# Moving the output blocks of two column tiles forward among the matmuls of a fused matmul and batch norm

## The chip, the cores and the metric

One core of a Trainium2 chip. The metric is the device time of one execution in microseconds (us); medians of several executions are quoted. Engines: PE is TensorE (matmuls and matmul transposes), DVE is VectorE, ACT is ScalarE, POOL is GpSimd, SP is SyncE, which issues the stores.

## The reference

```python
# x: 16 x 512 x 1024, weight: 1024 x 768, all float32
y = np.matmul(x, weight)                       # 8192 rows, 768 columns
mean = np.mean(y, axis=(0, 1), keepdims=True)  # per column, over all rows
var = np.var(y, axis=(0, 1), keepdims=True)
y_norm = (y - mean) / np.sqrt(var + eps)
return gamma * y_norm + beta
```

A column can be written only when all its 8192 rows are known. The kernel therefore works by column tiles of 128 (nt 0 to 5): a tile is multiplied, its statistics are closed, and it goes out while the next tiles are multiplied.

## The kernel before: the parts concerned

Rows come in 16 chunks of 512 (C = 16). The first phase loads x and computes nt 0 to 2 for all rows and nt 3 to 5 for the first five chunks (EARLY). After that nothing is loaded; nt 3, 4 and 5 are multiplied one after the other for the other eleven chunks. A result of nt 3 to 5 lies transposed (columns on the partitions), so it has to be normalised, turned back by PE, copied out of PSUM and stored. A block is two chunks: 1024 rows of one column tile, 512 KB.

```python
    def mm(nt, c, jws=range(JW), q0=0, q1=QPC):
        # [cut: bank]
        for jw in jws:
            for e in range(2):
                seq(nc.tensor.matmul(y_ps, w_sb[...], xT[c][...], ...))
                if turns:
                    turn_one()          # one waiting transpose after each matmul

    def finish(nt):
        seq(nc.vector.bn_aggr(mv[:, nt, :], stats[:, nt, :, :]))
        seq(nc.scalar.activation(std[:, one], mv[:, nt, 1:2], AF.Sqrt, bias=eps_sb, scale=1.0))
        # [cut: reciprocal, scale, shift]

    def out_copy(nts, m0, eng, late=False):
        while any(k == (nts, m0) for k, _, _ in turns):
            turn_one()                  # what is left of the block's 8 transposes, in a row
        # [cut: source; the target is a place in the ring, or an xT buffer when late]

    def outputs(nt, t0, step):
        for b in range(C // 2):
            tb = t0 + step * b
            for i in range(2):
                at(tb - 1.4 + 0.5 * i, norm, nt, 2 * b + i, "act" if tb < tr + 2.0 else "dve")
            at(tb, turn_y, (nt,), 2 * b * CH, 2 * RT)        # queue 8 transposes
            at(tb + 2.2, out_copy, (nt,), 2 * b * CH, "act")
            at(tb + 2.3, store, (nt,), 2 * b * CH, 2 * RT)

    for nt in range(GA, NT):            # GA = 3
        for c in range(EARLY, C):
            for jws in halves:
                unit(nt, c, MM_US / 2 + (0.12 if nt == GA else 0.17), jws)
        at(pe + 0.55, finish, nt)
        if nt == GA:
            outputs(nt, S + 40.0, 2.2)
        elif nt < NT - 1:
            outputs(nt, max(pe + 4.0, S + 55.0), 2.0)
        else:
            last_outputs(nt, pe + 3.0)
```

`at(t, ...)` gives a piece of work a planned time. All pieces are sorted by that time, and the sorted list is the order of instructions of each engine. The times are a plan only: on the chip an engine takes its instructions in that order, each as soon as what it waits for is there. `S` is the planned end of the first phase, `pe` the planned end of the tile's matmuls, `tr` the planned end of the row outputs of nt 0 to 2, which DVE and POOL normalise. The rule `tb < tr + 2.0` gives the earlier normalisations to ACT. The ring is one SBUF buffer for the data of most stores; a new piece waits until the store that used its place has landed.

## Time and profile before

| | before |
|---|---|
| median of the first runs | 223.6 us (223.54 to 223.75) |
| last matmul starts | 198.6 us |
| last copy out of PSUM ends | 212.5 us |
| last store lands | 220.3 us |

PE is busy without a hole up to the last matmul; the end is a queue of stores. Most lines of the profile that show this stand in the prediction. One more of the page, from its list of DMA issues (count, size, median us from issue to landing), is that of the last tile's large stores:

```profile
out_dram<-o_sb SPq DMA_DIRECT2D x7, 512.0 KB, 5.9
```

A lone store of that size lands after 2.9 us; the other 3.0 us it stands behind two more stores of 1.5 us each.

### The profile page before, as it was taken

To read this page: it belongs to the slowest core of one execution; us is meant where nothing else is said; L and a number is where in the kernel's file an instruction comes from. 1 tells how busy PE (TensorE), PEld (TensorE's weight loads), DVE (VectorE), ACT (ScalarE), POOL (GpSimd) and SP (SyncE) were. 2 spreads that over 40 slices of the span, in tenths; PEclk is the share of its full clock that TensorE was granted. 3 is DMA by queue.
4 is the path that set the end of the run, shared out by engine and by line. 5 is a ranking of instruction groups with operands and counts; after the bars stand their busy time and mean duration, and the time that the engine had idled before them with its cause. 6 is when DMAs were issued, how large, how long until landed. Compare 5 with 4: busy or idle time off the path is not lost.

```text
span 221.4 us, 3354 instructions
## 1 busy us (share of the span) xinstructions
PE 201.3 (91%) x1166; PEld 104.0 (47%) x1166; DVE 150.9 (68%) x260; ACT 117.5 (53%) x207; POOL 122.5 (55%) x145
## 2 busy tenths in 40 slices
PE   7669999999999999999999999999999999996510
PEld 3344555444545456465465544454444555555300
DVE  3222878897778888888634389778977568558930
ACT  2001553533554556465466217878879976858500
POOL 8897595964678689655069005996999300003000
PEclk9979999999999999999999999999999999997965
DMA  5999999999999999990000002898899998978995
GB/s 60 176 197 175 196 196 196 197 197 196 194 190 196 197 195 196 196 182 4 0 0 4 0 0 104 320 337 312 310 340 341 330 272 254 302 228 260 346 347 164
DMA packets 70049, 43.74 MB, mean 198 GB/s; under 512 B 3984, under 2 KB 69520, under 8 KB 70032
## 3 DMA queue, kind: packets, MB, share of 16 engines
q0 software_dynamic: 34624, 18.36, 60.6%
q1 hardware_dynamic: 35408, 25.18, 35.2%
q8 instruction: 9, 0.15, 0.3%
q14 instruction: 8, 0.07, 0.1%
HBM read 36.71 MB, written 25.17 MB: 280 GB/s over the span
## 4 chain that ended last, share of the span: by engine, by line
PE 84%; DMA 4%; DVE 3%; ACT 2%; issue 1%; POOL 1%; DVEq 0%; ACTq 0%; POOLq 0%
PE y_ps L189 52%; PE y_ps L179 23%; PE o_ps L336 7%; DMA ring<-in_x_dram 4%; DVE o_sb L351 1%; ACT o_sb L349 1%; POOL ring L155 1%; DVE y_sb L320 1%; ACT y_sb L315 1%; PE a_ps L262 1%; PE tot_ps L225 1%; ACT ring L349 0%; DVE xT_sb L167 0%; DVE stats L295 0%; ACT y_sb L298 0%
## 5 line engine op out<-in xcount | busy, mean ns | idle before, releaser
L189 PE MATMUL y_ps<-xT_sb,w_sb 128*128 128x512 bf16 (+1 forms) x540 | 133.0, 386 | 3.8 <-DVE xT_sb L167 1.9
L189 PEld LDWEIGHTS <-w_sb 128*128 128x128 bf16 x540 | 52.0, 97 | 69.7 <-issue 5.8
L295 DVE BATCH_NORM_STATS2 stats<-y_ps 128x6 f32<-128x512 f32 x66 | 45.0, 689 | 32.0 <-PE y_ps L189 31.8
L298 ACT CAST y_sb<-y_ps 128x512 bf16<-128x512 f32 x66 | 38.7, 586 | 52.2 <-DVE stats L295 49.5
L155 POOL DMA_DIRECT2D ring<-in_x_dram x72 | 45.3, 635 | 14.1 <-DVE xT_sb L167 7.4
L179 PE MATMUL y_ps<-w_sb,xT_sb 128*128 128x384 bf16 x320 | 53.1, 326 | 0.0
L336 PE MATMUL o_ps<-ident,y_sb 128*128 128x128 bf16 x264 | 45.5, 227 | 4.9 <-DVE y_sb L320 2.6
L167 DVE STREAM_TRANSPOSE xT_sb<-ring 128x1024 f32<-128x1024 f32 (+1 forms) x34 | 39.3, 1167 | 12.1 <-DMA ring<-in_x_dram 12.1
L205 POOL TENSOR_TENSOR sum<-sum,sq_sb 128x384 f32<-128x384 f32 x32 | 32.1, 1003 | 22.5 <-ACT sq_sb L201 21.3
L276 POOL TENSOR_TENSOR ring<-ring,sum 128x768 f32<-128x768 f32 x20 | 36.1, 1843 | 15.2 <-DVE ring L270 14.9
L179 PEld LDWEIGHTS <-xT_sb 128*128 128x128 bf16 x320 | 31.3, 98 | 21.6
L349 ACT CAST ring<-o_ps 128x1024 f32<-128x1024 bf16 (+1 forms) x28 | 25.8, 925 | 12.6 <-ACT y_sb L298 5.9
L208 DVE TENSOR_TENSOR sum<-y_ps,sum 128x384 f32<-128x384 f32 x40 | 21.8, 546 | 13.7 <-ACT sq_sb L201 13.1
L336 PEld LDWEIGHTS <-y_sb 128*128 128x128 bf16 x264 | 22.9, 101 | 9.9 <-DVE y_sb L320 6.0
L201 ACT ACTIVATE sq_sb<-y_ps 128x384 f32<-128x384 f32 x40 | 19.5, 493 | 13.1 <-PE y_ps L179 10.7
L214 ACT CAST y_sb<-y_ps 128x384 bf16<-128x384 f32 x40 | 19.0, 476 | 6.4 <-DVE sum L208 6.2
L270 DVE TENSOR_TENSOR ring<-y_sb,a_ps 128x768 f32<-128x768 bf16 x20 | 18.7, 938 | 0.0
L320 POOL TENSOR_SCALAR y_sb<-y_sb,scale,shift 128x512 bf16<-128x512 bf16 x2 | 1.7, 846 | 28.0 <-DVE shift L309 28.0
L315 ACT ACTIVATE y_sb<-y_sb,shift,scale 128x512 bf16<-128x512 bf16 x21 | 16.3, 816 | 0.0
L320 DVE TENSOR_SCALAR y_sb<-y_sb,scale,shift 128x512 bf16<-128x512 bf16 x43 | 16.1, 424 | 0.0
L148 PE MATMUL idle_ps<-idle_sb 128*128 128x512 bf16 x26 | 7.1, 441 | 1.2 <-DVE idle_sb L99 1.2
L142 POOL DMA_DIRECT2D w_sb<-in_weight_dram x12 | 6.1, 513 | 0.5 <-issue 0.2
(47 smaller groups left out, 36.3 us busy)
## 6 DMA issues: line engine op xcount, KB each, us to landing
ring<-in_x_dram POOLq DMA_DIRECT2D x56, 256.0 KB, 8.7
out_dram<-ring SPq DMA_DIRECT2D x32, 384.0 KB, 3.3
out_dram<-ring SPq DMA_DIRECT2D x16, 512.0 KB, 3.0
out_dram<-o_sb SPq DMA_DIRECT2D x7, 512.0 KB, 5.9
ring<-in_x_dram POOLq DMA_DIRECT2D x16, 128.0 KB, 5.2
w_sb<-in_weight_dram POOLq DMA_DIRECT2D x8, 96.0 KB, 4.5
w_sb<-in_weight_dram POOLq DMA_DIRECT2D x4, 192.0 KB, 5.1
out_dram<-o_sb SPq DMA_DIRECT2D x2, 256.0 KB, 4.7
```

Source lines behind the costliest of these rows:

```text
L155: seq(nc.gpsimd.dma_start(x_bf[32 * i:32 * i + 32], src[:, :, KQ * i:KQ * (i + 1)]))
L167: seq(nc.vector.transpose(dst[:, half, :, jw0:jw1], src[:, :, jw0:jw1]))
L179: seq(nc.tensor.matmul(y_ps, xT[c][:, jw, s * P:(s + 1) * P, e], w_sb[:, jw, e, 0:NA], start=(jw == 0 and e == 0), stop=(jw == JW - 1 and ...
L189: seq(nc.tensor.matmul(y_ps, w_sb[:, jw, e, nt * P:(nt + 1) * P], xT[c][:, jw, q0 * QR:q1 * QR, e], start=(jw == 0 and e == 0 and q0 == 0) ...
L205: seq(eng.tensor_add(acc, acc, py.pop(("sq", c, s))))
L208: seq(nc.vector.tensor_add(sum1, py["row", c, s][:, 0:NA], sum1))
L276: seq(nc.gpsimd.tensor_add(o_sb, o_sb, sum1[:, None, :].to_broadcast([P, 2, NA])))
L295: seq(nc.vector.bn_stats(stats[:, nt, i, :], py[nt, c]))
L298: seq(nc.scalar.copy(y(nt, c), py.pop((nt, c))))
L320: seq((nc.vector if eng == "dve" else nc.gpsimd).tensor_scalar(y(nt, c), y(nt, c), scale[:, nt:nt + 1], shift[:, nt:nt + 1], op0=ALU.mult, ...
L336: seq(nc.tensor.transpose(dst, src, ident))
L349: seq(nc.scalar.copy(o_sb, src))
```

## The change

The outputs of nt 3 begin 4 us of plan earlier and at closer steps; those of nt 4 begin right after its statistics, 6.5 us of plan earlier, and thus overlap those of nt 3. The intent: more of the transposes and stores lie beside matmuls, and less is left for the end.

```diff
         if nt == GA:
-            outputs(nt, S + 40.0, 2.2)
+            outputs(nt, S + 36.0, 1.95)
         elif nt < NT - 1:
-            outputs(nt, max(pe + 4.0, S + 55.0), 2.0)
+            outputs(nt, pe + 3.6, 1.85)
```

## The prediction

> **What bounds the kernel now.** I read the page's busy line first, then a table of stretches, the waits, the chain of work that ended last, and last the timelines of ScalarE (ACT) and of the stores. Three stretches matter: 162 to 178 us, where the outputs of the fourth column tile (nt 3) begin; 178 to 199 us, up to the last matmul; and the end.
>
> ```profile
> PE 201.3 (91%) x1166; PEld 104.0 (47%) x1166; DVE 150.9 (68%) x260; ACT 117.5 (53%) x207; POOL 122.5 (55%) x145
> ...
> 162.00:170.00 8.00, 7.96 (x47) 3.71 (x46) 6.04 (x9) 6.86 (x12) 8.00 (x6) 1.00 0.97 358
> 170.00:178.00 8.00, 8.00 (x59) 4.32 (x58) 5.13 (x14) 7.91 (x13) 3.53 (x2) 1.00 1.00 345
> 178.00:199.00 21.00, 21.00 (x158) 11.51 (x156) 13.18 (x31) 14.59 (x20) 0.00 (x0) 1.00 0.86 259
> 199.00:205.00 6.00, 4.02 (x41) 3.14 (x38) 5.25 (x12) 4.64 (x8) 1.68 (x2) 0.74 0.89 266
> 205.00:222.00 17.00, 3.45 (x40) 2.26 (x40) 7.04 (x14) 2.99 (x3) 0.00 (x0) 0.70 0.91 274
> ```
>
> The columns of the stretches are length, then busy time of PE, PE weight loads, DVE, ACT and POOL, then granted clock, DMA share and GB/s. PE is busy without a hole to 199 us, so until there every matmul or transpose that is added moves the last matmul. ACT is full (7.91 of 8.00) from 170 to 178, and has room (14.59 of 21.00) after it. From 205 on no engine is full, but the DMA is: the chain of work and the stores show the end.
>
> ```profile
> PEld L336 <- ACT y_sb L315: 0.5, 2, 0.4
> ...
> 198.75 0.24 PE y_ps L189
> 199.02 0.70 DVE stats L295
> 199.72 0.31 DVE y_sb L320
> 200.03 0.51 DVE mv L302
> 200.56 0.30 ACT std L303
> 201.42 1.13 DVE y_sb L320 x2
> ...
> SPq L538 <- DMA out_dram<-o_sb: 4.2, 3, 1.5
> ...
> L354 SPq DMA_DIRECT2D out_dram<-o_sb x9: 522/1390/1719, 203.7 to 214.4; - x9
> ```
>
> The first line is what PE waits for ACT's normalisations today: 0.5 us. The next six are the last matmul, its statistics, one normalisation of nt 4 that stands between them and the aggregate, the standard deviation, and the first normalisation of the last tile (nt 5) at 201.42. The chain then goes through transposes and copies and ends with a copy at 212.5, nine microseconds before the end: the rest is stores. The nine stores of nt 5 are issued from 203.7 to 214.4, though the last copy was there at 212.5: an issue stretches to 1.4 us where 0.37 is usual. At the very end the stores land 1.5 us apart (4.2 us in 3 waits, longest 1.5). 512 KB (0.524 MB) in 1.5 us is 347 GB/s, the full rate of this window. Store by store, the last two of nt 4 (issued 202.27 and 203.19) land at 206.7 and 208.2, and those of nt 5 follow without a gap: 208.9, 209.7, 211.2, and so on every 1.5 us to 220.3. So the end is a DMA queue that begins with work of nt 4.
>
> ```profile
> 168.30 1.52 ACT L315 ACTIVATE y_sb<-y_sb,shift,scale 128x512 bf16<-128x512 bf16 x2
> 169.73 0.57 ACT L298 CAST y_sb<-y_ps 128x512 bf16<-128x512 f32 x1
> 170.19 1.53 ACT L315 ACTIVATE y_sb<-y_sb,shift,scale 128x512 bf16<-128x512 bf16 x2
> 171.62 0.57 ACT L298 CAST y_sb<-y_ps 128x512 bf16<-128x512 f32 x1
> 172.08 1.02 ACT L349 CAST ring<-o_ps 128x1024 f32<-128x1024 bf16 x1
> 172.99 1.53 ACT L315 ACTIVATE y_sb<-y_sb,shift,scale 128x512 bf16<-128x512 bf16 x2
> ```
>
> Read start to start, because instructions on ACT overlap at their ends: a normalisation (L315) holds ACT 0.715 us (1.43 for two), a copy out of a matmul bank (L298) 0.46, an output copy (L349) 0.91, and one of 768 columns 0.69.
>
> **What the Trainium skill says.** "TensorE: Matmul & The Clock Gate", Back-to-back issue gap, gives columns over 2.4 GHz plus 2.5 ns for a lone warm matmul, thus some 56 ns for 128 columns, and a slower 81 ns sustained with weight loads. In this trace a pair of a 512-column matmul and a transpose takes 0.281 us where the matmul alone takes 0.226: a transpose costs 0.055. Five transposes in a row between two matmuls take 0.50 less 0.226, also 0.055 each, so runs of them are no dearer here. "Advanced Engine Details and Errata", Sequencer Loop, has engine instructions pushed into a queue and waiting there for their semaphores; I read it as in order, and the trace agrees (at 164.33 a transpose that waits for ACT holds the matmul behind it, 0.43 us between starts). "DMA: Bandwidth & Descriptors", Anatomy of one DMA, gives a fixed cost of about 2.0 us plus bytes over 436 GB/s. The trace has 2.9 us for a lone store of 512 KB, 1.4 fixed and 1.5 for the bytes; I use the trace.
>
> **The change part by part.** No instruction's work is added or taken away; the order changes. I counted it in the built kernels.
>
> (a) Transposes of nt 4. Before, 17 of its 64 come after the last matmul, where they lie beside the statistics and cost nothing. After, all come before it, and the last 20 matmuls run bare. That is 17 x 0.055 = +0.94 us to the last matmul.
>
> (b) The normalisation of nt 4 between the last statistics and the aggregate is gone: -0.31.
>
> (c) ACT between 164 and 178 us. The rule that gives a normalisation to ACT depends on the planned time, so four more of nt 3's go to ACT (ten, not six); and up to nt 4's standard deviation two more output copies stand in its order. 4 x 0.715 + 2 x 0.91 = 4.7 us more work in a stretch where ACT has next to no room. I walked both orders side by side. ACT from 163.89, where the orders part, never idle: the normalisations of chunks 0 and 1 end at 166.1, chunk 2 at 167.3, chunk 3 at 168.7; then a bank copy and two output copies; chunk 4 at 171.5, chunk 6 at 174.3, chunk 8 at 177.1. PE: the first two blocks of transposes find their chunks ready. PE reaches the third block at 170.26 and waits for chunk 4 to 171.5: 1.25 us. Eight pairs later (2.25 us) it is at 173.8 and waits for chunk 6 to 174.35: 0.55. Then 176.6, and chunk 8: 0.55 again. Chunks 10 on are DVE's, ready in time. Sum about +2.35 us. As PE has no hole later, it isn't made good.
>
> (d) Buffers. The output ring is shared by all stores, so the order of its reuse changes. A store of row tiles is now behind the first store of nt 3 in SyncE's order, and lands some 2.5 us later; the last row normalisation on DVE waits for its place, I reckon from 170 to 174. DVE has idle time there, and the bank it should free isn't wanted for eight allocations. No cost.
>
> (e) The end. With nt 4's stores all landed, nt 5's find an empty queue. Relative to the statistics, the first copy may now start at once on ACT, which before was busy with two output copies of nt 4 till 203.16. In the old times the stores of nt 5 would be issued at 203.0, 203.65, 205.35, 206.0, 207.8, 208.15, 210.25, 210.6 and 212.6. Each lands 1.5 us (0.75 for the two small ones) after the later of the landing before it and its issue + 1.43. The third lands at 205.35 + 1.43 + 1.5 = 208.3, and six more at 1.5 us make 217.3, against 220.3: -3.0. The same rule gives the landings of before to 0.1 us.
>
> Sum: +0.94 - 0.31 + 2.35 - 3.0 = 0.0 us. The gain is real and is given back by PE.
>
> **The rivals.** First, ACT keeps up (the waits of (c) don't appear). For it: only some tenths of slack decide each wait, and the schedule was drawn up so that ACT's work should fit. Against it: 7.91 of 8.00 busy today. Then the sum is -2.4, 221.2 us. Second, the ACT queue is worse than I walked it: the output copies wait for ring places (the waits show ACT before L349 at a few tenths each), each wait delays the normalisations behind it, and PE pays one for one; 1.5 us more gives 225.1. Third, the DMA end is no better: an instruction fetch on one DMA engine at 202.9 lies in the old tail, where the store issued at 202.27 took 4.4 us to land and not 2.9. If it comes at the same place and holds nt 5's stores, 0.7 of the 3.0 is lost, 224.3. I think it mostly falls before their data. Fourth, the gain shows nowhere because compute bounds the end: the last copy at 212.5 plus 2.9 would be 215.4, earlier than 217.3, so no.
>
> **Range and chances.** Before is 223.6. The sum of 0.0 has its largest error in (c), between 0 and 4 us, and that is lopsided: the walk could miss slack as easily as waits. A tuned kernel's author has some reason to try this, which I weigh by a tenth downward: 223.5. Eight in ten: 221.6 to 225.4, nearly the first two rivals. Two per cent is 4.5 us; faster by so much needs more than (b) and (e) together hold, slower needs 4.5 us more of waits: 3% each, 94% within.
>
> **What would show it.** (a) no transpose of nt 4 after the last matmul, and the last twenty matmuls 0.226 apart. (c) PE transposes waiting for ACT's L315 by 2 to 3 us between 168 and 178, in two to four waits, up from 0.5; the last matmul starting near 201.9 and not 198.6 (199.5 if ACT keeps up). (b) statistics followed at once by the aggregate. (e) first store of nt 5 issued 4.0 to 4.5 us after the last matmul starts (5.1 before); the last landing 18.5 us after it starts (21.7 before). I am wrong if the last matmul comes before 200.5 or after 203.5, or if the tail after it shortens by less than 2 us.

## The result, and the profile after

After: 223.85 us (223.72 to 224.05, 4 runs). Before, in the same comparison: 223.57 us (223.04 to 223.75, 4 runs). The ratio is 1.0017, 95% interval 0.9998 to 1.0036: the same. A ratio is the mean time of one kernel's fast runs over that of the other's in the same rounds, so it is not quite the ratio of the two medians.

The sum is nil, but the profile is not the same. First the table of stretches of the changed kernel, with the columns told in the prediction:

```profile
162.00:170.00 8.00, 7.96 (x56) 4.09 (x55) 5.45 (x8) 8.00 (x13) 8.00 (x5) 1.00 0.89 330
170.00:178.00 8.00, 6.15 (x42) 2.92 (x40) 3.91 (x5) 8.00 (x12) 3.84 (x3) 1.00 0.85 289
178.00:199.00 21.00, 21.00 (x167) 11.94 (x164) 14.26 (x37) 16.67 (x24) 0.11 (x1) 1.00 1.10 339
199.00:205.00 6.00, 3.70 (x18) 1.36 (x15) 3.20 (x9) 3.08 (x6) 0.00 (x0) 1.00 0.60 180
205.00:222.00 17.00, 7.52 (x64) 6.30 (x64) 10.28 (x18) 4.21 (x5) 1.68 (x2) 0.52 0.82 248
```

ACT is now full for 16 us, and PE has a hole: 6.15 of 8.00 between 170 and 178, where it had 8.00. Nothing after it makes that good, as PE is full again to the last matmul. The waits of the changed kernel between 160 and 205 us (engine, line, what it waited for: us in all, times, longest) name the cause:

```profile
DVE ring L270 <- DMA out_dram<-ring: 4.9, 2, 3.9
...
PEld L336 <- ACT y_sb L315: 3.3, 4, 1.4
...
PE o_ps L336 <- ACT y_sb L315: 1.9, 3, 1.1
```

L336 is a transpose, L315 a normalisation on ACT. Both the weight load and the transpose wait, so the two lines tell of the same waits and are not to be added. The spacing of the single matmuls in the trace gives three: 1.26 us at 170.5, 0.54 at 174.0 and 0.54 at 176.8, together 2.34 us. The first line is DVE's wait for a place in the ring, 3.9 us at one go. The ACT timeline at that time has no gap between its instructions:

```profile
168.99 0.58 ACT L298 CAST y_sb<-y_ps 128x512 bf16<-128x512 f32 x1
169.45 1.72 ACT L349 CAST ring<-o_ps 128x768 f32<-128x768 bf16 x2
171.05 1.54 ACT L315 ACTIVATE y_sb<-y_sb,shift,scale 128x512 bf16<-128x512 bf16 x2
172.47 0.59 ACT L298 CAST y_sb<-y_ps 128x512 bf16<-128x512 f32 x1
```

The pair of normalisations that begins at 171.05 is that of chunks 4 and 5, and the transposes of chunk 4 are what PE has waited for since 170.7.

The chain of work that ended last, from the last transposes of nt 4 on:

```profile
199.09 3.63 PE y_ps L189 x16
202.71 0.02 issue
202.74 0.71 DVE stats L295
203.45 0.02 issue
203.47 0.60 DVE mv L302
...
204.94 1.13 DVE y_sb L320 x2
```

Sixteen matmuls take 3.63 us, 0.227 each: no transpose among them. The aggregate (L302) follows the statistics at once; the normalisation that stood between them is gone. And the stores of the last tile no longer queue behind others. From the page, and from the waits of SP:

```profile
out_dram<-o_sb SPq DMA_DIRECT2D x7, 512.0 KB, 3.8
...
SPq L538 <- DMA out_dram<-o_sb: 3.3, 3, 1.5
```

3.8 us from issue to landing, not 5.9.

**A measure with less noise.** Up to the last of four small matmuls that spread the scale over the partitions (L262, at some 132 us) the two kernels are the same, but their first phase varies from run to run by a microsecond and more: in the traces that matmul starts between 131.4 and 135.2. So I also give, from each trace, D: from the start of the last spreading matmul to the end of the span, and its two parts, to the start of the last matmul and from there to the end (the tail).

| | last spreading matmul | to the last matmul | tail | D |
|---|---|---|---|---|
| before | 132.46 | 66.13 | 22.77 | 88.91 |
| after | 132.88 | 69.43 | 19.64 | 89.07 |
| difference | | +3.30 | -3.13 | +0.16 |

How far single traces agree: in the four whose order up to the last matmul is the same (before, e3, e8 and e11 below), the first part of D is 66.11 to 66.13. Three microseconds were gained and three were paid.

### The profile page after: what moved, and what is told of

It reads as the page before. It is cut to its first block, busy times and chain, and to the rows that moved or that the text cites. A ratio compares the mean times of both kernels' runs of the same rounds, so it can differ in the third digit from the quotient of the medians.

```text
span 221.9 us, 3358 instructions
## 1 busy us (share of the span) xinstructions
PE 203.2 (92%) x1166; PEld 105.4 (48%) x1166; DVE 151.1 (68%) x256; ACT 119.8 (54%) x211; POOL 122.3 (55%) x145
## 4 chain that ended last, share of the span: by engine, by line
PE 84%; DMA 4%; DVE 4%; ACT 3%; issue 1%; POOL 1%; DVEq 0%; ACTq 0%; POOLq 0%
PE y_ps L189 52%; PE y_ps L179 23%; PE o_ps L336 7%; DMA ring<-in_x_dram 4%; DVE o_sb L351 2%; ACT y_sb L315 2%; DVE y_sb L320 1%; ACT ring L349 1%; POOL ring L155 1%; PE a_ps L262 1%; PE tot_ps L225 1%; DVE xT_sb L167 0%; DVE stats L295 0%; DVE mv L302 0%; ACT y_sb L298 0%
## 5 line engine op out<-in xcount | busy, mean ns | idle before, releaser
L336 PE MATMUL o_ps<-ident,y_sb 128*128 128x128 bf16 x264 | 45.2, 239 | 7.3 <-DVE y_sb L320 5.4
L336 PEld LDWEIGHTS <-y_sb 128*128 128x128 bf16 x264 | 24.3, 107 | 13.2 <-DVE y_sb L320 6.9
L315 ACT ACTIVATE y_sb<-y_sb,shift,scale 128x512 bf16<-128x512 bf16 x25 | 19.4, 821 | 0.0
L349 ACT CAST o_sb<-o_ps 128x1024 f32<-128x1024 bf16 (+1 forms) x5 | 4.2, 842 | 5.8 <-PE o_ps L336 5.8
```

The lines of the kernel that those rows point to most:

```text
L315: seq(nc.scalar.activation(y(nt, c), y(nt, c), AF.Identity, bias=shift[:, nt:nt + 1], scale=scale[:, nt:nt + 1],))
L336: seq(nc.tensor.transpose(dst, src, ident))
L349: seq(nc.scalar.copy(o_sb, src))
```

## The experiments

Twelve kernels were run. In the table, time and ratio are against the kernel before in the same rounds; the median of that kernel was between 223.0 and 224.0 us on the various occasions. The expectations of e5 to e8 count D from the start of the third spreading matmul instead of the last, 0.4 us earlier; so 89.3 for the kernel before stands there for 88.9 here, and 0.4 is to be taken off their other values of D.

| | kernel | median us | ratio (95%) | to last matmul | tail | D |
|---|---|---|---|---|---|---|
| e1 | only nt 3 moved | 225.65 | 1.0121 (1.0074 to 1.0168) | 68.48 | 22.79 | 91.27 |
| e2 | only nt 4 moved | 221.90 | 0.9963 (0.9903 to 1.0023) | 67.06 | 19.58 | 86.64 |
| e3 | before, two stores left out | 220.78 | 0.9895 (0.9845 to 0.9946) | 66.11 | 19.80 | 85.91 |
| e4 | after, three stores issued later | 223.74 | 1.0032 (0.9986 to 1.0077) | 69.43 | 19.43 | 88.86 |
| e5 | nt 4 moved, one block late | 221.07 | 0.9877 (0.9835 to 0.9920) | 66.62 | 19.58 | 86.20 |
| e6 | nt 4 moved, two blocks late | 222.16 | 0.9926 (0.9890 to 0.9961) | 66.18 | 21.18 | 87.35 |
| e7 | e6, engines exchanged in nt 5 | 221.79 | 0.9918 (0.9882 to 0.9954) | 66.18 | 21.25 | 87.42 |
| e8 | before, engines exchanged in nt 5 | 223.41 | 0.9986 (0.9947 to 1.0026) | 66.11 | 23.10 | 89.20 |
| e9 | after, nt 3 normalised by DVE | 224.61 | 1.0012 (0.9979 to 1.0045) | 70.17 | 19.64 | 89.81 |
| e10 | e6, 12 more dummy matmuls at the start | 220.94 | 0.9858 (0.9833 to 0.9883) | 66.17 | 19.68 | 85.86 |
| e11 | before, 12 more dummy matmuls | 222.03 | 0.9919 (0.9889 to 0.9949) | 66.12 | 21.69 | 87.81 |
| e12 | after, four normalisations left out | 224.01 | 1.0011 (0.9982 to 1.0040) | 69.31 | 19.63 | 88.94 |

All gave the right result but e3 and e12. The theory is that of the prediction.

### e1 and e2: one half of the change at a time

```diff
 e1:
-            outputs(nt, S + 40.0, 2.2)
+            outputs(nt, S + 36.0, 1.95)
 e2:
-            outputs(nt, max(pe + 4.0, S + 55.0), 2.0)
+            outputs(nt, pe + 3.6, 1.85)
```

> Only the fourth column tile's outputs are moved forward; the fifth tile's stay as before. Theory (ScalarE's four extra normalisations hold TensorE, and the end is the queue of stores left by the fifth tile): the three waits of transposes for ScalarE of 1.26, 0.54 and 0.54 us appear as in the changed kernel, nothing is gained at the end, since the fifth tile's last two stores still stand there; 223.6 + 2.35 = 225.9 us, last matmul some 2.3 us later than before. Rival (moving the fourth tile is harmless, and the loss comes from the overlap of both tiles or from the transposes pulled before the last matmul): 223.6 us within 0.5, waits for ScalarE near 0.5 us in all.

> Only the fifth column tile's outputs are moved forward; the fourth's stay as before, so the two overlap more. Theory: 17 transposes more before the last matmul (+0.94), one normalisation less on the way to the statistics (-0.31), the queue of stores empty at the end (-3.0), no added waits for ScalarE: 221.2 us. Rival (the overlap of the two tiles makes the copies wait for places in the ring or for each other, and TensorE with them): 223 us or more, with new waits of transposes or of output copies between 180 and 199 us.

Moving nt 3 alone costs 2.36 us of D, nearly all of it before the last matmul (68.48 against 66.13), and the three waits are there again, 1.26, 0.54 and 0.54 us. Moving nt 4 alone gains 2.27 us of D: +0.93 before the last matmul, -3.19 in the tail. Added, the two halves give +0.09, and the whole change has +0.16. So the halves are independent, one good and one bad, and the overlap of the two tiles is not the trouble. By time e2's gain is not clear of noise (its interval includes 1, one of its four runs took 223.81 us): the trace of e2 had a first phase 1.1 us longer than that of before. There the verdict rests on D, from one trace of each kernel.

### e3: the queue at the end

```diff
-            at(tb + 2.3, store, (nt,), 2 * b * CH, 2 * RT)
+            if not (nt == 4 and b >= 6):
+                at(tb + 2.3, store, (nt,), 2 * b * CH, 2 * RT)
```

> The kernel before without the last two stores of the fifth tile (the result is wrong on purpose: these rows are not written). All of its compute stays. Theory (the old end is a queue of stores that begins with these two): 3.0 us less, 220.6 us, the last copy still at some 212.5 us and the last landing near 217.3. Rival one (the copies of the last tile set the end): no change, 223.6 us. Rival two (the instruction fetch on one DMA engine at 202.9 us holds the first stores of the last tile): 221.3 us.

D falls by 3.00 us, without any change to the work of the engines. That the end of the old kernel was a queue beginning with these two stores is shown; the copies, whose last ends no earlier, don't set it. What made that queue so long is not separated here: with the two stores their bytes go, and also whatever held them up (see e11).

### e4: the wait for the ring

```diff
-            at(tb + 2.3, store, (nt,), 2 * b * CH, 2 * RT)
+            at(tb + (4.1 if nt == GA and b < 3 else 2.3), store, (nt,), 2 * b * CH, 2 * RT)
```

> The changed kernel with the first three stores of the fourth tile put later in SyncE's order, so that stores of row tiles are not held behind them. Theory (the 3.95 us that VectorE waits for a place in the ring lie in its idle time): that wait falls to below 2 us, the three waits of TensorE for ScalarE and the time stay, 223.85 us within 0.4. Rival (this wait of VectorE is what delays ScalarE's copies and so TensorE): the waits of TensorE shrink and the time falls by 1 us or more.

DVE's wait for the ring falls from 4.9 to 0.8 us in all. PE's three waits stay to a hundredth, as does the time to the last matmul, 69.43. In the changed kernel the ring's wait costs nothing; e12 below shows that this is only half of the truth.

### e9 and e12: what ACT's queue is made of

In e9 all normalisations of nt 3 go to DVE (with e4's order of stores, so that DVE need not wait for the ring). In e12 the four normalisations are left out which the change gave to ACT in addition.

```diff
 e9:
-                at(tb - 1.4 + 0.5 * i, norm, nt, 2 * b + i, "act" if tb < tr + 2.0 else "dve")
+                at(tb - 1.4 + 0.5 * i, norm, nt, 2 * b + i, "dve")
 e12:
+                if not (nt == GA and b in (3, 4)):
                     at(tb - 1.4 + 0.5 * i, norm, nt, 2 * b + i, "act" if tb < tr + 2.0 else "dve")
```

> The changed kernel with all normalisations of the fourth tile on VectorE (0.36 us each there) in place of ten on ScalarE, and the first three stores of that tile later in SyncE's order as in e4. Theory (TensorE's three waits of 1.26, 0.54 and 0.54 us come from ScalarE's queue being full with these normalisations): all three are gone, 2.3 us less than the changed kernel; from the last spreading matmul to the end 86.7 us where the changed kernel has 89.1. Rival (the data come late by any engine, as VectorE waits for the ring and stands in order too): waits of the same size for VectorE, 88.5 us or more.

> The changed kernel without the normalisations of chunks 6 to 9 of the fourth tile, the four that the change gave to ScalarE in addition (the result is wrong on purpose: these chunks go out unnormalised). Theory (they fill ScalarE and cause the second and third wait; the first comes from the four that were moved up): the wait of 1.26 us stays, the two of 0.54 are gone, 1.1 us less than the changed kernel, 88.0 us from the last spreading matmul to the end (89.1 there). Rival (ScalarE's copies alone keep TensorE waiting at this spacing): waits of about 0.5 us return at other places, 88.7 us or more.

Both miss. In e9 the rival is right: ACT's three waits are gone, and PE waits for DVE instead, at five places between 169 and 182 us with 0.36 to 0.70 each. The trace points to the duration of DVE's normalisations (groups of instructions, one shape each; busy us and mean ns of one), in e9 between 160 and 180 us:

```profile
L320 DVE TENSOR_SCALAR y_sb<-y_sb,scale,shift 128x512 bf16<-128x512 bf16 x12 | 10.5, 893 | 0.0
```

and in the kernel before, between 174 and 199 us:

```profile
L320 DVE TENSOR_SCALAR y_sb<-y_sb,scale,shift 128x512 bf16<-128x512 bf16 x25 | 9.0, 404 | 0.0
```

The single ones in e9 take up to 2.04 us while POOL shifts row outputs beside them. One of them with the add of POOL beside it:

```profile
170.94 1.93 POOL L276 TENSOR_TENSOR ring<-ring,sum 128x768 f32<-128x768 f32 x1 [1.09 <-DVE ring L270]
...
171.72 1.30 DVE L320 TENSOR_SCALAR y_sb<-y_sb,scale,shift 128x512 bf16<-128x512 bf16 x1
```

POOL ends at 172.87 and DVE at 173.02. The five of 1.3 us and more in e9 all end 0.15 us after the end of such an add; those that begin while POOL is idle take 0.40 us. The Trainium skill's page "SBUF — State Buffer" (Terms) describes a pair of SBUF ports for which DVE and GpSimd compete, locked for a whole instruction, so that the loser stands still; that fits these times, though no run here takes POOL's adds away. My 0.36 us was taken from a stretch in which POOL was idle.

In e12 the first wait, 1.26 us, stays and the two of 0.54 are gone, as expected. But a new one of 0.97 us comes at 180.3, and D falls by 0.13 us only. Its waits, between 160 and 200 us:

```profile
PEld L336 <- ACT y_sb L315: 1.8, 2, 1.4
PEld L336 <- DVE y_sb L320: 1.1, 1, 1.1
```

The new one is for DVE: it stood 3.9 us for the ring, closed nt 4's statistics late, and normalised chunk 12 of nt 3 behind that. In the changed kernel PE arrives at this point later by ACT's waits, and DVE is ready. So two causes lie in a row: take ACT's away and DVE's lateness costs nearly as much. That this lateness comes from the ring is read from the timeline; no run takes both waits away. That the four extra normalisations cause the second and third wait is shown; that leaving them with another engine would gain is not.

### e5 and e6: some of nt 4 after the last matmul

Transposes after the last matmul lie beside the statistics and are free. Could a block or two stay there, as long as their stores are out in time?

```diff
-            outputs(nt, max(pe + 4.0, S + 55.0), 2.0)
+            outputs(nt, pe + 3.6, 2.4, 1)      # e5; e6: outputs(nt, pe + 3.6, 2.5, 2)
...
+            if b >= C // 2 - late:             # the last ones
+                n = b - (C // 2 - late)        # mm_end: the planned end of all matmuls
+                tn, tb, tc = mm_end - 3.4 + n, mm_end + 0.05, 0.35 + 0.8 * n
+            else:
+                tn = tb - 1.4                  # tn: the normalisations, tb + tc: the copy
```

> Fourth tile's outputs as before; of the fifth tile's eight blocks seven among the matmuls and one right after the last matmul, with its normalisations done earlier. Theory (a transpose before the last matmul costs 0.055 us, after it nothing, as long as its store is out before the last tile's third store): 9 transposes more before the last matmul than in the kernel before (+0.5), -0.31 for the normalisation, -3.0 at the end: 2.8 us less than before, from the spreading matmuls (the line that spreads the scale) to the end 86.5 us where the kernel before has 89.3. Rival (any block left after the last matmul brings the queue of stores back): the end is no earlier than with only the fifth tile moved, 87.0 or more.

> As the one with one block late, but two blocks right after the last matmul, the first one's copy ahead of the standard deviation on ScalarE and the second's after it. Theory: 1 transpose more than before (+0.05), -0.31, +0.1 for the copy ahead of the standard deviation, -3.0: some 3.1 us less than before, 86.2 us from the spreading matmuls to the end. Rival (two blocks are 3.0 us of stores and come back at the end as in the kernel before): 88 us or more.

e5 gains 2.71 us of D where 2.8 was expected, and by time it is faster than the kernel before (0.9877; the changed kernel had 1.0017, in other rounds). To the last matmul the count of transposes before it decides: 183 of them (before) 66.13 us, 184 (e6) 66.18, 192 (e5) 66.62, 200 (e2) 67.06. The last less the first is 0.93 us for 17: 0.055 each, over four kernels. e6 misses: 1.56 us gained, not 3.1. Its second late store took 4.5 us to land where 2.9 is usual, and all after it came 1.5 us late.

### e10 and e11: who holds that store

At 203.3 us, 4.5 us after the last matmul, the trace of e6 has a packet of 16 KB on another queue, q8, which fetches instructions. In the kernel before it is at 202.9, 4.3 us after the last matmul, and there too a store took longer than it should (4.4 us). The Trainium skill, "Runtime: NRT & Kernel Launch" (Instruction fetch mechanics), says that instructions are refilled in blocks of 16 KiB by a DMA queue of the sequencer's own. The kernel before has nine such packets, and between the first and the last of them PE starts 257 matmuls and weight loads for each, which fits 256 instructions to a block. If the block is PE's, more PE instructions at the start move the fetch to an earlier point of the work.

```diff
-    WAKE = 26
+    WAKE = 38      # dummy matmuls that warm PE before x arrives; e10: in e6, e11: in the kernel before
```

> The kernel of e6 with 38 instead of 26 dummy matmuls at the very start (they end before TensorE has work, at some 11 us). What is asked: why the second late block of e6 landed 4.5 us after its issue, not 3.0. Theory: a 16 KB fetch of TensorE's instructions, 4.5 us after the last matmul, shares one DMA engine with that store and every later one lands 1.5 us late; 24 more instructions at the start bring the fetch some 24 instructions earlier, where few stores flow; then 1.5 us less than e6, 85.9 us from the last spreading matmul to the end (e6: 87.35). Rival (two blocks in flight are simply too many): as e6, 87.3 us.

> The kernel before with 38 dummy matmuls at the start. Theory (the fetch also holds the fifth tile's last two stores there, which took 4.4 and 5.0 us to land): the queue at the end is 1.5 us shorter, 87.4 us from the last spreading matmul to the end (before: 88.9). Rival (the queue is all bytes): 88.9 us.

The twelve matmuls and their weight loads are 24 instructions. The fetch now lies at 199.1 us in e10, 0.6 us before the last matmul, and at 197.8 in e11, 0.3 us after it. The store in question, alone in a narrow window, from issue to landing: in the kernel before (where it is the last but one of nt 4), in e6 and in e10.

```profile
out_dram<-ring SPq DMA_DIRECT2D x1, 512.0 KB, 4.4
```

```profile
out_dram<-ring SPq DMA_DIRECT2D x1, 512.0 KB, 4.5
```

```profile
out_dram<-ring SPq DMA_DIRECT2D x1, 512.0 KB, 2.9
```

e10 has D = 85.86 us, 85.9 expected; of the kernels with a right result it has the lowest D and the lowest time, 220.94 us, 1.4% below the kernel before (by time e5 is not clear of it). e11 gains 1.10 us, 1.5 expected. Its trace shows where the other 0.4 us went: the fetch now holds an earlier store of nt 4, issued at 196.8 us (4.7 us to landing), and the stores behind it have not quite caught up when the last but one of nt 4 is issued at 201.2: that one takes 3.35 us, not 2.9. The last of nt 4 and all of nt 5 follow behind it without a gap. That fetch and store share a DMA engine is the theory's reading; the runs show only that the store lands 1.5 us later where the fetch meets it. Twelve idle matmuls at the start of the old kernel gain more than the whole change.

### e7 and e8: an exchange that told nothing

In the last tile chunks 2 and 3 were given to DVE and ACT, chunks 4 and 5 to POOL and DVE, to have the third store out earlier.

```diff
-        ... ((1,), "v", "act"), ((2, 3), "gg", "dve"), ((4, 5), "vv", "act")]
+        ... ((1,), "v", "act"), ((2, 3), "vv", "act"), ((4, 5), "gg", "dve")]
```

> As the one with two blocks late, and in the last tile chunks 2 and 3 are normalised by VectorE and copied by ScalarE, chunks 4 and 5 by GpSimd and VectorE, so that the third store may go some 0.3 us earlier. Theory (with the queue empty the third store sets when all later ones land): 0.3 us less than the one with two blocks late. Rival (the copies of the last tile set the end): the same or longer.

> The kernel before with the same exchange in the last tile. Theory (its end is a full queue of stores from the fifth tile's on, so when the last tile's third store is issued is of no account): no change, 89.3 us from the spreading matmuls to the end, within 0.15. Rival: some 0.3 us less, as with two blocks late.

In e7 the third store was issued 6.42 us after the last matmul, in e6 6.35. The exchange did not do what it was for, and e6 turned out to have a queue of its own. Nothing follows, and whether an earlier third store helps is open. The trace of e8 is of a slow run (its first phase was 2.7 us longer); its fast times can't tell no change from 0.3 us less: the interval of the ratio is some 0.9 us wide to either side.

## Why the prediction was right

223.5 us was predicted with 221.6 to 225.4, and 223.85 came. The steps came out each by itself, so it was not luck of the sum; but one of them, (e), had the right size and only part of the cause:

- **(a) Transposes before the last matmul**, +0.94: the last sixteen matmuls run bare in the changed kernel (twenty had been said), and e2, with 17 more transposes and no new waits, has +0.93.
- **(b) The normalisation before the aggregate**, -0.31: from the start of the last statistics to the aggregate it was 1.01 us (199.02 to 200.03) and is 0.73 (202.74 to 203.47), -0.28.
- **(c) PE waits for ACT**, +1.25, 0.55 and 0.55: 1.26, 0.54 and 0.54 us in the changed kernel, the same in e1. The step rests on three durations read start to start from a timeline and on the order of instructions. The text names four normalisations and two copies as the cause; e12 confirms the four for the second and third wait. For the first, e9 shows only that it goes when all ten leave ACT; what the two copies add is not tested.
- **(d) The ring costs nothing**: true in the changed kernel (e4). The step was too simple, however: DVE's wait for the ring comes right behind ACT's, and in e12, without ACT's second and third, PE waits 0.97 us for DVE.
- **(e) The end**, -3.0: the tail is 3.13 us shorter (e2: 3.19). In the changed kernel the last landing is 18.5 us after the last matmul, 21.7 before, as predicted; the first store is issued 4.1 us after it, within the 4.0 to 4.5 given. The cause was only half seen. The prediction says that its rule gives the old landings to 0.1 us. It does so from 206.7 us on, but by the rule the store issued at 202.27 lands at 205.2, and it landed at 206.7. These 1.5 us are the fetch of e10 and e11. So of the 3.0 us about half is the bytes of nt 4's late stores, and half is that the fetch no longer meets them (an estimate: 1.1 us gained in e11, and the 0.4 that its trace explains). e3 takes both away at once. The granted clock was lower in the changed kernel's tail (0.52 between 205 and 222 us, 0.70 before), and its last copy ended 14.6 us after the last matmul, not 13.9; as the stores set the end, that cost nothing.

Of the rivals, ACT keeping up is refuted by the waits. Ring waits that delay ACT are refuted by e4. The third, an instruction fetch in the way of the stores, was judged harmless for the changed kernel, and it cost nothing there. But it did not wholly fall before the data, as the prediction thought: the fetch is at 206.9 us, and the first store of nt 5, issued at 206.5, landed after 2.9 us, where the same store of 256 KB took 2.2 in e3. The third store, from which on the landings are back to back, was issued at 208.9 and landed after 2.9 us, as a lone one of 512 KB does. That the fetch fell so early had not been worked out, and was in part luck. Where it meets a late store of nt 4 it costs 1.5 us (e6 against e10).

Where I was wrong is in what would mend the change. Giving the normalisations to DVE (e9) looked free by DVE's busy share and was not, by the duration beside POOL.

## What to carry to other kernels

When a change moves much and the time stays, split it: here one half gains 2.3 us and the other loses 2.4, and keeping only the good half has a D of 86.6 us, less than either kernel (88.9 and 89.1). On an engine that has no hole, each wait that another engine's queue puts into its order is paid in full, so before pulling work forward, walk the order of the engine that feeds it, with durations taken from a stretch with the same neighbours. Work after the last matmul is free only as long as its store is out before the last tile's stores. And when a store lands late with nothing queued ahead of it, look at the other DMA queues before blaming the bytes.

## What the Trainium skill lacked or had wrong

- "TensorE: Matmul & The Clock Gate", Back-to-back issue gap, gives 81 ns sustained for 128 columns with weight loads and about 131 ns for 512. Neither was met here, at full granted clock: between 512-column matmuls a transpose costs 55 ns (0.93 us for 17, e2), and 512-column matmuls with their weight loads start 227 ns apart (sixteen in 3.63 us).
- "DMA: Bandwidth & Descriptors", Anatomy of one DMA, gives its formula (2.0 us plus bytes over 436 GB/s) for DMAs issued by GpSimd. For a store issued by SyncE no page was found to have one. A lone 512 KB store here lands after 2.9 us, and in a full queue one lands every 1.5 us.
- "Runtime: NRT & Kernel Launch", Instruction fetch mechanics, calls the cost of a fetch mostly hidden. It was hidden for the engine that fetches, but not for the stores: a store in flight at that time landed after 4.4 or 4.5 us, not 2.9, and 24 more instructions at the start took it away (e10).
- "SBUF — State Buffer", Terms, has the port that DVE and GpSimd share and the loser that stands still, with which these runs agree; no page was found to give a time for this pair of instructions. Normalising 128x512 bf16 on DVE took 1.3 to 2.0 us beside POOL's adds and 0.40 us with POOL idle (e9).
